# Spreading the splits of the down-projection operands, and handing Strassen sums from bank to bank on ScalarE

## The chip, the core and the metric

The kernel runs on one NeuronCore of a Trainium2 chip. Its engines are TensorE (matrix products, with a separate queue of weight loads), VectorE and ScalarE (elementwise work; both can read and write PSUM, the eight accumulator banks that TensorE writes), GpSimd (here it only issues DMAs) and SyncE (it only issues DMAs). In the rows they are PE, PEld, DVE, ACT, POOL and SP. The metric is the device time of one execution in microseconds, as the median of several runs.

## What is computed

The reference is a trunk of two layers on 1024 tokens of width 1024. Each layer has a mixer (a state-space branch and a windowed attention branch, merged by gates) and then a dense SwiGLU feed-forward part of width 2816:

```
hn2 = rmsnorm(h, norm2_g[layer])
ff = jax.nn.silu(hn2 @ ffn_w_gate[layer]) * (hn2 @ ffn_w_up[layer])
h = h + ff @ ffn_w_down[layer]
```

The change touches this feed-forward part alone.

## The kernel before, in words

**Numbers.** Every fp32 operand is split into a high part, rounded by a ScalarE copy to the type fp32r, and a low part, the rest, by a VectorE subtraction (`split`, `quad_part`, `parts`). A product then takes three matmuls of 128x128 by 128x512: high by high, high by low, low by high. The two token halves are h = 0 and 1, of 512 columns each.

**Quads.** Most of the feed-forward part is done in quads: a 2x2 block product by Strassen's seven products instead of eight. In a gate quad (`quad_items`) the two block rows are the gate and the up weights of one 128-row slice f, the two block columns are the token halves, and each product sums over four 128-deep tiles: 12 matmuls. In a down quad (`down_quad`) the block rows are two neighbouring output slices m and m+1, and the sum runs over half of a chunk of slices f: chunks of 8 give 12 matmuls in a product, chunks of 6 give 9. Layer 0 has 14 gate quads and 4+2 down quads in 2 chunks; layer 1 has 19 gate quads and 4+4+2 down quads in 3 chunks: 33 and 16 in all.

The weights of a quad come as five parts a to e (`quad_part`): a is the upper row as loaded, the others are sums and differences made by VectorE. Parts a and b hold two products' weights, in buffers `whi` and `wlo` (three of each); c, d and e hold one, in slots `whs` and `wls`. The other operands are the tiles of the normalized input with their Strassen sums `T[0]` to `T[3]` (gate quads), or seven sets `b11`, `t0`, `t1`, `b21`, `t2`, `t3`, `b22` of a chunk (down quads).

**Banks.** The seven products of a quad go to PSUM banks named x, y, v and w. Before, their order was x(a), y(b), v(b), x(a), y(c), w(d), v(e), with the first product of the next quad set in ahead of the last. What a bank shares with others was added on VectorE: `first` copies x to an SBUF tile (ScalarE), `second` adds y to it, `third` adds y and v, further adds bring in w and the finished v. All SBUF tiles of 128x512 come from one pool of 86 slots (`A`), all banks from one pool of 8 (`PS`).

**Operands of the down quads.** As a gate quad ends, `keep` and `row` write its results and their Strassen sums to DRAM. Round the start t0 of a chunk (counted in products), `op_load` reads a set back (SyncE's queue) and `op_split` splits it. `SETS` gives the order; the loads were put at t0-12 to t0-2, the splits at t0-4 to t0+2, one set for each product. While a chunk begins, the sets of the one before (or the operands of the gate quads) still hold their slots until their last product.

**Order of work.** `ffn_items` writes out one list of items: products, epilogues, loads and splits. The weights' splits are set in between by a look-ahead (`emit`, `ahead`). From that list a scheduler of the language fixes, before the run, each engine's own order, so engines run their queues in order and wait for one another by semaphores; it may move an instruction ahead of older ones that it thinks will not be ready.

Of the kernel before, what the change touches and what calls it, by code (L numbers as in the profile page):

```python
# [8 lines left out]
F32 = mybir.dt.float32  # L9
F32R = mybir.dt.float32r  # L10
# [3 lines left out]
ADD, SUB, MUL = ALU.add, ALU.subtract, ALU.mult  # L14
# [7 lines left out]
HC = 512  # L22
# [4 lines left out]
CHUNKS = (((8, 8), (16, 6)), ((0, 8), (8, 8), (16, 6)))  # L27
QUAD_FROM = (8, 3)
DOWN_QUADS = 2
SETS = ("b11", "t1", "t0", "b21", "t2", "t3", "b22")  # L30
QUAD_LOOK = 5
NEG = -1e30
EPS = 1e-6
# [65 lines left out]
class Trunk:  # L99
# [85 lines left out]
    def piece(self, ps, g, off, xs, start):  # L185

        from functools import partial
        mm = partial(self.nc.tensor.matmul, skip_group_check=not start)
        for k, (xh, xl) in enumerate(xs):
            s = off + k * P  # L190
            wh, wl = g.hi[:, s:s + P], g.lo[:, s:s + P]
            mm(ps, lhsT=wh, rhs=xh, start=start and k == 0, stop=False)  # L192
            mm(ps, lhsT=wh, rhs=xl, start=False, stop=False)  # L193
            mm(ps, lhsT=wl, rhs=xh, start=False, stop=k == len(xs) - 1)  # L194

    def item(self, fn, *granules):
        self.seq.append((fn, granules))
# [980 lines left out]
    def ffn_items(self, l, fill, head):  # L1178
# [19 lines left out]
        def keep(f, h, x):  # L1198

            if f < grouped:  # L1200
                ff[h][f] = self.split(x, f"ff{f % 6}")
                return
            c, j, k = places[f]
            act[f, h] = x
            if (k, h) != (0, 1) or c == len(chunks) - 1:
                put(c, f"b{k + 1}{h + 1}", j, x)

        def row(f):
            c, j, k = places[f]
# [12 lines left out]
        def op_load(c, kind):  # L1222
            ts = ops[c, kind] = [self.A("fr") for _ in range(chunks[c][1] // 2)]
            for j, t in enumerate(ts):
                nc.sync.dma_start(t, fd[c, kind, j])

        def op_split(c, kind):
            ops[c, kind] = [self.split(t, "fo") for t in ops[c, kind]]

        def gate(f, h, g, st, part=None):  # L1230
            if part != 1:
# [66 lines left out]
        def down_quad(c, m):  # L1298

            f0, n = chunks[c]  # L1300
            w = n * P // 2
            at_end = c == len(chunks) - 1
            q = Quad(*(self.t["w_down"][l, i, :, f0:f0 + n].rearrange("p k c -> p (k c)") for i in (m, m + 1)), w)
            b = {}

            def product(bank, g, off, kind, start):
                def run():
                    if start:
                        b[bank] = self.PS(f"q{bank}")
                    self.piece(b[bank], g, off, ops[c, kind], start)  # L1310
                return (run, g)

            p = [product(*a) for a in (("x", q.a, 0, "b11", True), ("y", q.b, w, "t1", True), ("v", q.b, 0, "t0", True),
                                       ("x", q.a, w, "b21", False), ("y", q.c, 0, "t2", False), ("w", q.d, 0, "t3", True),
                                       ("v", q.e, 0, "b22", False))]

            def out(i, h, x):
                if at_end:
                    last_sum(m + i, h, x)
                else:  # L1320
                    nc.gpsimd.dma_start(self.hs[m + i, h], x, accum_op=ADD)

            def first():
                b["p1"] = self.A("qp")
                nc.scalar.copy(b["p1"], b["x"])

            def second():
                b["u2"] = self.A("qu")
                V.tensor_tensor(b["u2"], b["p1"], b["y"], ADD)

            def c11():
                if at_end:
                    out(0, 0, b["x"])
                    return
                t = self.A("dx")
                nc.scalar.copy(t, b["x"])
                out(0, 0, t)

            def third():
                V.tensor_tensor(b["p1"], b["p1"], b["y"], ADD)  # L1340
                b["c22"] = self.A("qc")
                V.tensor_tensor(b["c22"], b["p1"], b["v"], ADD)
                out(1, 1, b["c22"])

            def c21():
                V.tensor_tensor(b["p1"], b["p1"], b["w"], ADD)
                out(1, 0, b["p1"])

            def c12():
                V.tensor_tensor(b["u2"], b["u2"], b["v"], ADD)  # L1350
                out(0, 1, b["u2"])

            return p, [(fn,) for fn in (first, second, c11, third, c21, c12)]

# [25 lines left out]
        def quad_items(f):  # L1380

            q = Quad(self.t["w_gate"][l, f].rearrange("p k c -> p (k c)"), self.t["w_up"][l, f].rearrange("p k c -> p (k c)"))
            b = {}

            def product(bank, g, off, xs, start):
                def run():
                    if start:
                        b[bank] = self.PS(f"q{bank}")
                    self.piece(b[bank], g, off, xs(), start)
                return (run, g)  # L1390

            B = lambda h, a: lambda: self.hn2[h][a:a + 4]
            p = [product("x", q.a, 0, B(0, 0), True), product("y", q.b, HC, lambda: T[1], True),
                 product("v", q.b, 0, lambda: T[0], True), product("x", q.a, HC, B(0, 4), False),
                 product("y", q.c, 0, lambda: T[2], False), product("w", q.d, 0, lambda: T[3], True),
                 product("v", q.e, 0, B(1, 4), False)]

            def first():
                b["p1"] = self.A("qp")
                nc.scalar.copy(b["p1"], b["x"])  # L1400

            def second():
                b["u2"] = self.A("qu")
                V.tensor_tensor(b["u2"], b["p1"], b["y"], ADD)
# [5 lines left out]
            def third():  # L1410
                V.tensor_tensor(b["p1"], b["p1"], b["y"], ADD)
                b["c22"] = self.A("qc")
                V.tensor_tensor(b["c22"], b["p1"], b["v"], ADD)

            def half0():
                s = b["s0"]
                V.scalar_tensor_tensor(s, s, 1.0, b["x"], ADD, MUL)
                V.tensor_tensor(b["p1"], b["p1"], b["w"], ADD)
                V.scalar_tensor_tensor(s, b["p1"], 0.5, s, MUL, MUL)  # L1419
                keep(f, 0, s)  # L1420

            def gate1():
                V.tensor_tensor(b["u2"], b["u2"], b["v"], ADD)  # L1423
                b["s1"] = self.A("ts")
                nc.scalar.activation(b["s1"], b["u2"], AF.Tanh, scale=0.5)  # L1425

            def half1():
                s = b["s1"]
                V.scalar_tensor_tensor(s, s, 1.0, b["u2"], ADD, MUL)
                V.scalar_tensor_tensor(s, b["c22"], 0.5, s, MUL, MUL)  # L1430
                keep(f, 1, s)
                row(f)

            return p, [(fn,) for fn in (first, second, gate0, third, half0, gate1, half1)]

# [53 lines left out]
        def at(t, fn):  # L1489
            more.setdefault(t, []).append((fn,))  # L1490

        for t0, c in begins:
            for k, kind in enumerate(SETS):
                at(t0 - 12 + k * 17 // 10, lambda c=c, kind=kind: op_load(c, kind))
                at(t0 - 4 + k, lambda c=c, kind=kind: op_split(c, kind))
        c = len(chunks) - 1
        end = 7 * len(made)

# [19 lines left out]

        do(made[0][0][0])
        for i, (p, e) in enumerate(made):  # L1520
            do(p[1])
            main.append(e[0])
            do(p[2])
            main.append(e[1])
            do(p[3])
            do(p[4])
            main.append(e[2])
            do(p[5])
            main.append(e[3])
            if i + 1 < len(made):  # L1530

                do(made[i + 1][0][0])
            main.append(e[4])
            do(p[6])
            main.extend(e[5:])
# [270 lines left out]
```

## Time and profile before

| | us |
|---|---|
| median of 3 runs (2644.98 to 2649.70) | 2648.95 |
| the profiled execution | 2647.83 |
| its span, first to last instruction | 2646.1 |
| TensorE busy in the span | 2564.8 (97%) |
| VectorE busy | 1827.9 (69%) |
| ScalarE busy | 1022.1 (39%) |

The profiled execution took 1.7 us more than its span, and is within 0.1% of the median. Busy shares are averages over stages; matmuls are pipelined, so a busy TensorE says nothing of its rate. Mean granted TensorE clock: 0.986 of full speed.

### The profile page before, as it was taken

The page shows a single profiled execution, that of the slowest core. Times are in us where ns is not written, and L with a number is a line of the kernel's source. Part 1 is how long each engine was busy: PE and PEld are TensorE (multiplying, and loading weights), DVE is VectorE, ACT ScalarE, POOL GpSimd, SP SyncE. Part 2 cuts the span into 40 slices and gives each one's busy share as a digit, 9 for nine tenths or more (in the row PEclk, how much of TensorE's full clock was granted, in tenths as well). Part 3 has the DMA queues.
Part 4 walks back from the last instruction along what each step waited for, and adds up shares of the span by engine and source line. Part 5 has one row for each costly group of instructions (what it writes and reads, how often), then busy time and mean ns, then how long its engine had stood idle before and what let it go on. Part 6 is the DMA issues. An engine that isn't in the chain of part 4 may idle for free.

```text
span 2646.1 us, 35134 instructions
## 1 busy us (share of the span) xinstructions
PE 2564.8 (97%) x12722; PEld 2088.1 (79%) x12722; DVE 1827.9 (69%) x3577; ACT 1022.1 (39%) x1949; POOL 321.3 (12%) x528
## 2 busy tenths in 40 slices
PE   8999899999999999998999999999999999998997
PEld 6787677887888888886787778888878888886776
DVE  9986878575977677677763465756377777676766
ACT  5336744422443333233444553453233222234432
POOL 0141011000142111011100001200001011111110
PEclk9999999999999999998999999999999999998998
DMA  3453435354174533255732244434322233255773
GB/s 139 136 186 118 136 120 180 124 186 140 55 197 132 98 110 108 96 202 137 200 133 76 72 140 161 159 120 167 127 92 93 102 104 116 92 199 156 176 190 123
DMA packets 160510, 357.01 MB, mean 135 GB/s; under 512 B 22048, under 2 KB 44832, under 8 KB 160336
## 3 DMA queue, kind: packets, MB, share of 16 engines
q1 hardware_dynamic: 117136, 236.28, 26.9%
q0 software_dynamic: 43200, 118.48, 15.9%
q8 instruction: 100, 1.64, 0.2%
q14 instruction: 74, 0.61, 0.1%
HBM read 230.97 MB, written 123.68 MB: 134 GB/s over the span
## 4 chain that ended last, share of the span: by engine, by line
PE 88%; DVE 7%; ACT 2%; issue 1%; DMA 1%; SPq 0%; DVEq 0%; ACTq 0%
PE pj L181 6%; PE pj L182 6%; PE pj L183 6%; PE qx L192 3%; PE qx L193 3%; PE qx L194 3%; PE qy L192 3%; PE qy L194 3%; PE qy L193 3%; PE qv L192 3%; PE qv L193 3%; PE qv L194 3%; PE wo L181 2%; PE wo L183 2%; PE wo L182 2%; PE br L181 2%
## 5 line engine op out<-in xcount | busy, mean ns | idle before, releaser
L181 PE MATMUL pj<-rah,whi 128*128 128x512 f32 x768 | 306.2, 399 | 0.4 <-DVE sm L804 0.4
L182 PE MATMUL pj<-ral,whi 128*128 128x512 f32 x768 | 300.1, 391 | 0.7 <-DVE ral L116 0.7
L183 PE MATMUL pj<-rah,wlo 128*128 128x512 f32 x768 | 299.9, 391 | 0.0
L170 DVE TENSOR_TENSOR wlo<-raw,whi 128x1024 fp32r<-128x1024 f32 (+1 forms) x126 | 145.7, 1156 | 168.3 <-ACT whi L169 159.0
L169 ACT CAST whi<-raw 128x1024 fp32r<-128x1024 f32 (+1 forms) x126 | 125.3, 995 | 273.9 <-PE pj L182 115.1
L181 PEld LDWEIGHTS pj<-rah,whi 128*128 128x128 f32 x768 | 144.7, 188 | 35.4 <-issue 4.7
L182 PEld LDWEIGHTS pj<-ral,whi 128*128 128x128 f32 x768 | 144.8, 189 | 30.9 <-DVE ral L116 2.6
L183 PEld LDWEIGHTS pj<-rah,wlo 128*128 128x128 f32 x768 | 144.5, 188 | 30.8
L1425 ACT ACTIVATE ts<-qu 128x512 f32<-128x512 f32 x33 | 20.9, 633 | 287.2 <-DVE qu L1423 287.2
L804 DVE CUSTOM_DVE_ANT_0 x<-s,bias,nsink 128x384 f32<-128x384 f32 (+1 forms) x128 | 67.5, 581 | 64.0 <-PE s L798 63.9
L1423 DVE TENSOR_TENSOR qu<-qu,qv 128x512 f32<-128x512 f32 x33 | 22.7, 687 | 125.8 <-PE qv L194 125.8
L192 PE MATMUL qx<-rfh,whi 128*128 128x512 f32 x264 | 102.7, 389 | 0.0
L193 PE MATMUL qx<-rfl,whi 128*128 128x512 f32 x264 | 102.7, 389 | 0.0
L194 PE MATMUL qx<-rfh,wlo 128*128 128x512 f32 x264 | 102.7, 389 | 0.0
L976 ACT COPY s5sg<-s5s 64x256 f32<-64x256 f32 x128 | 51.7, 404 | 128.8 <-DVE s5s L971 127.4
L181 PE MATMUL wo<-mgh,whi 128*128 128x512 f32 x256 | 100.0, 391 | 0.0
L1196 POOL DMA_DIRECT2D fd_b<-ts x60 | 32.6, 543 | 553.4 <-DVE ts L1419 464.2
L183 PE MATMUL wo<-mgh,wlo 128*128 128x512 f32 x256 | 99.7, 389 | 0.0
L182 PE MATMUL wo<-mgl,whi 128*128 128x512 f32 x256 | 99.6, 389 | 0.0
L157 ACT CAST whs<-s 128x512 fp32r<-128x512 f32 (+1 forms) x98 | 59.9, 612 | 99.3 <-DVE s L150 93.3
L157 ACT CAST whi<-sm 128x1024 fp32r<-128x1024 f32 (+1 forms) x49 | 50.6, 1033 | 122.7 <-PE qv L193 102.9
L158 DVE TENSOR_TENSOR wlo<-sm,whi 128x1024 fp32r<-128x1024 f32 (+1 forms) x49 | 58.9, 1202 | 41.8 <-ACT whi L157 41.7
(468 smaller groups left out, 7191.0 us busy)
## 6 DMA issues: line engine op xcount, KB each, us to landing
raw<-in_w_in SPq DMA_DIRECT2D x52, 512.0 KB
raw<-in_w_gate SPq DMA_DIRECT2D x44, 512.0 KB
raw<-in_w_up SPq DMA_DIRECT2D x44, 512.0 KB
fd_t<-ft POOLq DMA_DIRECT2D x72, 256.0 KB, 2.7
fr<-fd_t SPq DMA_DIRECT2D x72, 256.0 KB
g<-th POOLq DMA_DIRECT2D x64, 256.0 KB, 2.8
thr<-g SPq DMA_DIRECT2D x64, 256.0 KB
fd_b<-ts POOLq DMA_DIRECT2D x60, 256.0 KB, 2.3
```

The costliest lines, as they stand in the source:

```text
L157: nc.scalar.copy(g.hi[:, n], src)
L158: V.tensor_tensor(g.lo[:, n], src, g.hi[:, n].bitcast(F32), SUB)
L169: nc.scalar.copy(g.hi[:, :n], g.raw[:, :n])
L170: nc.vector.tensor_tensor(g.lo[:, :n], g.raw[:, :n], g.hi[:, :n].bitcast(F32), SUB)
L181: mm(ps, lhsT=wh, rhs=xh, start=k == 0, stop=False)
L182: mm(ps, lhsT=wh, rhs=xl, start=False, stop=False)
L183: mm(ps, lhsT=wl, rhs=xh, start=False, stop=k == n - 1)
L192: mm(ps, lhsT=wh, rhs=xh, start=start and k == 0, stop=False)
L193: mm(ps, lhsT=wh, rhs=xl, start=False, stop=False)
L194: mm(ps, lhsT=wl, rhs=xh, start=False, stop=k == len(xs) - 1)
L804: V.tensor_tensor_reduce(out=x[:, :n], in0=ps[:, :n], in1=self.bias[hd][:, bo:bo + n], op0=ADD, op1=ALU.min, scale=-1.0, scalar=self.nsink ...
L976: nc.scalar.copy(SG[64 * r:64 * r + 64, g * 256:(g + 1) * 256].rearrange("p (d n) -> p d n", d=2), Sv[64 * g:64 * g + 64, :, r])
```

## The change

Four edits, all in the feed-forward part.

1. A loaded operand tile is split in place: the tile that the DMA filled becomes the low part, so a split takes one new slot, not two with the loaded one freed later.
2. The seven sets are taken in the order in which the products use them; loads go to t0-14 to t0-2 and splits to t0-10 to t0+3 by two explicit lists, 13 products from the first split to the last instead of 6.
3. Each quad has five banks x, v, y, z, w. ScalarE copies x into y before T1's product accumulates on it, then y into z and v into an SBUF tile, then y into w. The products accumulate on these copies. VectorE is left with one add for c22 and one for c12 (or the up value of half 1).
4. The order of products is x, v, y, x, y, z, (next x), w, and the epilogues are moved with it: c21 and half 0 come last.

```diff
-SETS = ("b11", "t1", "t0", "b21", "t2", "t3", "b22")
+SETS = ("b11", "t0", "t1", "b21", "t2", "b22", "t3")
+LOADS = (-14, -10, -8, -7, -5, -4, -2)
+SPLITS = (-10, -6, -4, -2, 0, 2, 3)
...
+    def carry(self, b):
+        nc, V = self.nc, self.nc.vector
+        def first():
+            b["y"] = self.PS("qy")
+            nc.scalar.copy(b["y"], b["x"])
+        def second():
+            b["z"] = self.PS("qz")
+            nc.scalar.copy(b["z"], b["y"])
+            b["sv"] = self.A("qp")
+            nc.scalar.copy(b["sv"], b["v"])
+        def third():
+            b["w"] = self.PS("qw")
+            nc.scalar.copy(b["w"], b["y"])
+            b["c22"] = self.A("qc")
+            V.tensor_tensor(b["c22"], b["sv"], b["y"], ADD)
+        return first, second, third
...
-            ts = ops[c, kind] = [self.A("fr") for _ in range(chunks[c][1] // 2)]
+            ts = ops[c, kind] = [self.A("fol", F32R) for _ in range(chunks[c][1] // 2)]
...
-            ops[c, kind] = [self.split(t, "fo") for t in ops[c, kind]]
+            for lo in ops[c, kind]:
+                hi = self.A("foh", F32R)
+                nc.scalar.copy(hi, lo.bitcast(F32))
+                V.tensor_tensor(lo, lo.bitcast(F32), hi.bitcast(F32), SUB)
...
-("y", q.b, w, "t1", True), ("v", q.b, 0, "t0", True),
-("x", q.a, w, "b21", False), ("y", q.c, 0, "t2", False), ("w", q.d, 0, "t3", True), ("v", q.e, 0, "b22", False)
+("v", q.b, 0, "t0", True), ("y", q.b, w, "t1", False),
+("x", q.a, w, "b21", False), ("y", q.c, 0, "t2", False), ("z", q.e, 0, "b22", False), ("w", q.d, 0, "t3", False)
...
             def c21():
-                V.tensor_tensor(b["p1"], b["p1"], b["w"], ADD)
-                out(1, 0, b["p1"])
+                if at_end:
+                    out(1, 0, b["w"])
+                    return
+                t = self.A("dx")
+                nc.scalar.copy(t, b["w"])
+                out(1, 0, t)
...
             def half0():
                 V.scalar_tensor_tensor(s, s, 1.0, b["x"], ADD, MUL)
-                V.tensor_tensor(b["p1"], b["p1"], b["w"], ADD)
-                V.scalar_tensor_tensor(s, b["p1"], 0.5, s, MUL, MUL)
+                V.scalar_tensor_tensor(s, b["w"], 0.5, s, MUL, MUL)
                 keep(f, 0, s)
+                row(f)
...
-            for k, kind in enumerate(SETS):
-                at(t0 - 12 + k * 17 // 10, lambda c=c, kind=kind: op_load(c, kind))
-                at(t0 - 4 + k, lambda c=c, kind=kind: op_split(c, kind))
+            for kind, a, b in zip(SETS, LOADS, SPLITS):
+                at(t0 + a, lambda c=c, kind=kind: op_load(c, kind))
+                at(t0 + b, lambda c=c, kind=kind: op_split(c, kind))
```

## Rows read from the trace of the kernel before

**Rows 1.** The page: busy us, share of the span and instructions of each engine.
```profile
PE 2564.8 (97%) x12722; PEld 2088.1 (79%) x12722; DVE 1827.9 (69%) x3577; ACT 1022.1 (39%) x1949; POOL 321.3 (12%) x528
```
**Rows 2.** TensorE's waits, whole span: us in total, times, longest.
```profile
PE qw L193 <- DVE fol L116: 14.8, 5, 6.3
PE qw L192 <- ACT foh L115: 13.5, 5, 3.2
...
PE qv L192 <- DVE qc L1413: 5.5, 2, 2.8
```
**Rows 3.** Timeline of TensorE, start of layer 0's first chunk: start, duration, [idle before].
```profile
1202.22 0.39 PE L194 MATMUL qv<-foh,wlo 128*128 128x512 f32 x1
1205.37 0.78 PE L192 MATMUL qv<-rfh,whs 128*128 128x512 f32 x1 [2.77 <-DVE qc L1413]
...
1212.00 0.60 PE L192 MATMUL qw<-foh,whs 128*128 128x512 f32 x1 [2.01 <-ACT foh L115]
1218.84 0.79 PE L193 MATMUL qw<-fol,whs 128*128 128x512 f32 x1 [6.24 <-DVE fol L116]
...
1224.30 0.39 PE L194 MATMUL qw<-foh,wls 128*128 128x512 f32 x1
```
**Rows 4.** Windows: length; busy (instructions) PE, PEld, DVE, ACT, POOL; clock, DMA share, GB/s.
```profile
908.00:1099.00 191.00, 191.00 (x844) 158.19 (x844) 139.17 (x200) 61.00 (x93) 22.89 (x37) 1.00 0.39 113
1202.22:1224.30 22.08, 11.07 (x31) 7.89 (x30) 19.03 (x31) 11.01 (x21) 3.25 (x6) 0.69 0.30 112
1294.34:1304.53 10.19, 6.38 (x15) 4.37 (x14) 8.38 (x14) 6.92 (x13) 0.00 (x0) 0.67 0.50 125
2389.66:2411.92 22.26, 11.14 (x32) 8.00 (x30) 19.23 (x31) 11.01 (x21) 3.25 (x6) 0.69 0.31 112
2484.01:2494.27 10.26, 6.18 (x20) 4.41 (x18) 10.17 (x17) 7.28 (x14) 0.86 (x1) 0.83 0.22 27
2564.31:2574.41 10.10, 6.29 (x16) 4.28 (x14) 8.38 (x14) 6.92 (x13) 0.00 (x0) 0.66 0.54 143
```
**Rows 5.** Timeline of ScalarE, the same start of layer 0's first chunk.
```profile
1202.42 1.04 ACT L157 CAST whi<-sm 128x1024 fp32r<-128x1024 f32 x1 [2.79 <-PE qv L193]
1203.37 2.17 ACT L115 CAST foh<-fr 128x512 fp32r<-128x512 f32 x4
```
**Rows 6.** Timeline of VectorE, the same start.
```profile
1203.49 1.22 DVE L158 TENSOR_TENSOR wlo<-sm,whi 128x1024 fp32r<-128x1024 f32 x1 [2.29 <-ACT whi L157]
1204.63 0.68 DVE L1413 TENSOR_TENSOR qc<-qp,qv 128x512 f32<-128x512 f32 x1
...
1218.10 2.49 DVE L116 TENSOR_TENSOR fol<-fr,foh 128x512 fp32r<-128x512 f32 x4
```
**Rows 7.** Windows of two gate quads and of two down quads.
```profile
1099.00:1137.00 38.00, 38.00 (x170) 31.46 (x169) 27.70 (x41) 10.71 (x16) 4.33 (x8) 1.00 0.33 112
1233.00:1271.00 38.00, 38.00 (x170) 31.46 (x168) 20.17 (x28) 10.21 (x16) 6.86 (x8) 1.00 0.80 190
```
**Rows 8.** Groups by line and shape: busy us, mean ns, idle before.
```profile
L157 ACT CAST whi<-sm 128x1024 fp32r<-128x1024 f32 x45 | 47.3, 1051 | 95.4 <-PE qv L193 91.4 <-issue 2.6 <-PE dn L182 1.4
L1400 ACT COPY qp<-qx 128x512 f32<-128x512 f32 x33 | 18.8, 569 | 1.4 <-PE qx L194 1.4
L157 ACT CAST whi<-sm 128x768 fp32r<-128x768 f32 x4 | 3.3, 836 | 27.2 <-issue 15.7 <-PE qv L193 11.5
```
**Rows 9.** Timeline of TensorE: the last matmul of one gate quad's first product.
```profile
1101.40 0.39 PE L194 MATMUL qx<-rfh,wlo 128*128 128x512 f32 x1
```
**Rows 10.** Timeline of ScalarE in that gate quad.
```profile
1105.27 0.63 ACT L1425 ACTIVATE ts<-qu 128x512 f32<-128x512 f32 x1 [9.26 <-DVE qu L1423]
1105.80 0.57 ACT L1400 COPY qp<-qx 128x512 f32<-128x512 f32 x1
```
**Rows 11.** Waits of SyncE's DMA queue, whole span.
```profile
SPq L1225 <- PE qy L194: 6.7, 6, 2.3
SPq L1225 <- PE qx L194: 4.9, 5, 1.7
```

More of the change, by code (lines that the diff above doesn't have):

```diff
@@ L1222, in op_load @@
         def op_load(c, kind):
-            ts = ops[c, kind] = [self.A("fr") for _ in range(chunks[c][1] // 2)]
+            ts = ops[c, kind] = [self.A("fol", F32R) for _ in range(chunks[c][1] // 2)]
             for j, t in enumerate(ts):
-                nc.sync.dma_start(t, fd[c, kind, j])
+                nc.sync.dma_start(t.bitcast(F32), fd[c, kind, j])
         def op_split(c, kind):
-            ops[c, kind] = [self.split(t, "fo") for t in ops[c, kind]]
+            pairs = []
+            for lo in ops[c, kind]:
+                hi = self.A("foh", F32R)
+                nc.scalar.copy(hi, lo.bitcast(F32))
+                V.tensor_tensor(lo, lo.bitcast(F32), hi.bitcast(F32), SUB)
+                pairs.append((hi, lo))
+            ops[c, kind] = pairs
         def gate(f, h, g, st, part=None):
@@ L1311, in product @@
                 return (run, g)
-            p = [product(*a) for a in (("x", q.a, 0, "b11", True), ("y", q.b, w, "t1", True), ("v", q.b, 0, "t0", True),
-                                       ("x", q.a, w, "b21", False), ("y", q.c, 0, "t2", False), ("w", q.d, 0, "t3", True),
-                                       ("v", q.e, 0, "b22", False))]
+            p = [product(*a) for a in (("x", q.a, 0, "b11", True), ("v", q.b, 0, "t0", True), ("y", q.b, w, "t1", False),
+                                       ("x", q.a, w, "b21", False), ("y", q.c, 0, "t2", False), ("z", q.e, 0, "b22", False),
+                                       ("w", q.d, 0, "t3", False))]
             def out(i, h, x):
@@ L1321, in out @@
                     nc.gpsimd.dma_start(self.hs[m + i, h], x, accum_op=ADD)
[L1323 to L1329, printed above, removed]
+            first, second, carry = self.carry(b)
             def c11():
@@ L1339, in third @@
             def third():
-                V.tensor_tensor(b["p1"], b["p1"], b["y"], ADD)
-                b["c22"] = self.A("qc")
-                V.tensor_tensor(b["c22"], b["p1"], b["v"], ADD)
+                carry()
                 out(1, 1, b["c22"])
             def c21():
-                V.tensor_tensor(b["p1"], b["p1"], b["w"], ADD)
-                out(1, 0, b["p1"])
+                if at_end:
[4 more added lines that the diff above has]
+                out(1, 0, t)
             def c12():
-                V.tensor_tensor(b["u2"], b["u2"], b["v"], ADD)
-                out(0, 1, b["u2"])
+                u = self.A("qu")
+                V.tensor_tensor(u, b["sv"], b["z"], ADD)
+                out(0, 1, u)
             return p, [(fn,) for fn in (first, second, c11, third, c21, c12)]
@@ L1392, in quad_items @@
             B = lambda h, a: lambda: self.hn2[h][a:a + 4]
[L1393 to L1404, printed above, removed]
+            p = [product("x", q.a, 0, B(0, 0), True), product("v", q.b, 0, lambda: T[0], True),
+                 product("y", q.b, HC, lambda: T[1], False), product("x", q.a, HC, B(0, 4), False),
+                 product("y", q.c, 0, lambda: T[2], False), product("z", q.e, 0, B(1, 4), False),
+                 product("w", q.d, 0, lambda: T[3], False)]
+            first, second, third = self.carry(b)
             def gate0():
@@ L1408, in gate0 @@
                 nc.scalar.activation(b["s0"], b["x"], AF.Tanh, scale=0.5)
[L1410 to L1413, printed above, removed]
             def half0():
@@ L1417, in half0 @@
                 V.scalar_tensor_tensor(s, s, 1.0, b["x"], ADD, MUL)
[L1418 to L1419 removed]
+                V.scalar_tensor_tensor(s, b["w"], 0.5, s, MUL, MUL)
                 keep(f, 0, s)
+                row(f)
             def gate1():
[L1423 removed]
+                b["u2"] = self.A("qu")
+                V.tensor_tensor(b["u2"], b["sv"], b["z"], ADD)
                 b["s1"] = self.A("ts")
@@ L1431, in half1 @@
                 keep(f, 1, s)
-                row(f)
             return p, [(fn,) for fn in (first, second, gate0, third, half0, gate1, half1)]
@@ L1520, in ffn_items @@
         for i, (p, e) in enumerate(made):
+            main.append(e[0])
             do(p[1])
-            main.append(e[0])
             do(p[2])
@@ L1525, in ffn_items @@
             do(p[3])
+            main.append(e[2])
             do(p[4])
-            main.append(e[2])
+            main.append(e[3])
             do(p[5])
-            main.append(e[3])
             if i + 1 < len(made):
                 do(made[i + 1][0][0])
-            main.append(e[4])
+            main.append(e[5])
             do(p[6])
-            main.extend(e[5:])
+            main.extend(e[6:] + [e[4]])
         assert not more, more.keys()
```

## The prediction

> **What bounds the kernel now.** I read the page's busy shares first, then TensorE's waits, then a timeline where those waits lie, and last windows over each of them. TensorE is busy for 97% of the span [rows 1], so only the time in which it stands still or runs slowly can be won; the change takes no matmul away. Of the waits, the longest belong to one place: the first product on bank w, five times on VectorE's low parts and five times on ScalarE's high parts, and twice product v of the last gate quad [rows 2]. Together 14.8 + 13.5 + 5.5 = 33.8 us. Five is the number of chunk starts.
>
> One start in detail: TensorE begins its last full-speed matmul at 1202.22, waits 2.77, 2.01 and 6.24 us, and is back at full pace at 1224.30 [rows 3]. The reader is to see that matmuls after a wait come slower too (0.78 and 0.79 us against 0.39). So I price a start by its whole stretch. In a steady stretch 844 matmuls take 191.00 us, 0.226 each, at clock 1.00; in the five stretches 30, 14, 30, 18 and 14 began (the weight loads count them), at clocks 0.66 to 0.83 [rows 4]. At the steady pace they need 6.79, 3.17, 6.79, 4.07 and 3.17 us; they took 22.08, 10.19, 22.26, 10.26 and 10.10. Lost: 15.3 + 7.0 + 15.5 + 6.2 + 6.9 = 50.9 us, of which 33.8 is waiting and 17.1 the slower clock behind it. That is 1.9% of the run, and the ceiling of what the change can win there.
>
> Why TensorE waits: VectorE works 19.03 of the 22.08 us [rows 4] and still ends splits of a set at 1220 [rows 6]. In the rest of its time it is blocked by order: ScalarE's cast of part b can't start before TensorE lets its buffer go (1202.42, [rows 5]); VectorE's `wlo` waits 2.29 us for that cast; and the add c22, for which TensorE waits, stands behind it [rows 6].
>
> **The spread of the splits.** A product of 12 matmuls takes 12 x 0.226 = 2.72 us, one of 9 takes 2.04. Four splits take VectorE 2.49 us [rows 6], a start's seven sets 17.4. Two gate quads keep VectorE busy 27.70 of 38 us, 73%; two down quads 20.17, 53% [rows 7]. Old plan, from t0-4 to t3's product at t0+7: 11 products or 29.9 us, demand 10.9 x 0.73 + 19.0 x 0.53 + 17.4 = 35.4. It is 5.5 us short, and blocking adds to that. New plan, from t0-10 to t0+7: 17 products or 46.2 us. VectorE loses three adds in each quad; at some 0.60 us each (four splits in 2.49 us give 0.60 from start to start) two quads fall to 24.1 and 16.6 us, 63% and 44%. Demand 27.2 x 0.63 + 19.0 x 0.44 + 17.4 = 42.9: it fits, at 93%. With the old adds it would be 27.2 x 0.73 + 19.0 x 0.53 + 17.4 = 47.3 and would not: the two halves of the change need each other. In the densest part, t0-6 to t0+4, six sets fall in 27.2 us: 14.9 + 16.3 x 0.63 + 10.9 x 0.44 = 30.0, 2.8 us over; each set is used three to nine products after its split is listed, so I cost this at nothing. Without that lead it is 2.8 us at each of the two starts behind gate quads, 5.6.
>
> The wait on c22 goes away for another reason: no product accumulates on v once it has been read, so TensorE needs nothing of that add.
>
> **The copies.** ScalarE gets three more copies a quad (z, the saved v, w), and one for c21 in the 12 down quads that aren't at the end: 3 x 49 + 12 = 159. A copy from PSUM to SBUF takes 0.569 us [rows 8]. From PSUM to PSUM no row shows; bounds are 0.48 (four casts in 2.17 us, 0.52 apart [rows 5], less the copy's 0.05) and 1.05, the cast of twice the size [rows 8]. I take 0.57, the nearest row; 91 us in all on an engine that is busy 39% [rows 1]. Beside the splits: two gate quads rise from 10.71 to 14.1 us of 38, two down quads from 10.21 to about 14.8 [rows 7]; in the 46.2 us round a start 27.2 x 0.37 + 19.0 x 0.39 + 7 x 2.18 = 32.8, 71%. It fits.
>
> What counts is not load but lateness, as TensorE now waits for these copies. x into y has the products w and v as cover, 5.4 us; y into w has z and the next x, 5.4 us; y into z has only the second x product, 2.72 us (2.04 in the last chunks), since T2's product overwrites y. Ahead of it stands one cast of part a or b, whose buffer comes free with the same product: 1.05 + 0.57 = 1.62 us, under 2.72; in the small chunks 0.84 + 0.57 = 1.41, under 2.04 [rows 8]. With the upper price of the copy 2.10 and 1.89, still under. So in a steady quad the copies cost nothing, and the work that hides them is the one product in between; without that cover each costs its 0.57 to 1.05.
>
> At a start the set b22 is listed right behind the first quad's y product, in front of this copy: 4 casts in 2.17, 1.05 and 0.57 make 3.79 us, 1.07 over; for 3 tiles 3 x 0.52 + 0.10 + 0.84 + 0.57 = 3.07, 1.03 over. Five starts: 3 x 1.07 + 2 x 1.03 = 5.3 us. Below it, nothing, if the scheduler sets the copy first. I double it to 10 for the orders that a busy share can't show.
>
> **Order, queues and memory.** The loads are as many as before, 28 or 21 a start, and stand in SyncE's queue with the weights' loads. Some already wait for a slot, 6.7 us in six cases and 4.9 in five, at most 2.3 us [rows 11]. By my count of slots the old operands hold 56 of 86; with loads and splits in place the new plan reaches 72 at t0-7 (the old one 68 at t0-9), and the quads' own tiles take about 20 more. So some loads will wait for a product to end: one or two products late, and the weights' loads queued behind them with them, whose buffers hold a quad ahead (19 us). Nothing, on a lead of three to nine products; if it costs, it is the partial case below. `row` moves behind half 0, some 1.2 us later, and its writes in GpSimd's queue with it; they are read several quads later. c21 at the end reads its bank directly, an add fewer.
>
> **Sum.** 50.9 - 10 = 41 us less. The profiled execution's 2647.8 would become 2607; the median of the runs stands 1.1 us above that execution, so 2648.95 becomes 2608. The bounds: nothing left at the starts, 2598; 20 left, 2618.
>
> **Rivals.**
>
> *Half of the loss stays.* The slots are the limit, loads come late, and splits pile up before t0 again. For it: the slot count above, and a VectorE at 93%. Against: loads wait at most 2.3 us today. Half of 50.9 is 25: 2623, in a range of 2618 to 2643.
>
> *Slower: ScalarE's y-to-z copy comes late in every quad.* Today's copy of x starts at 1105.80, though its product's last matmul ended at 1101.79: 4.0 us late, because it stands behind the tanh of the quad before, and that waits for VectorE [rows 9, 10]. The Trainium skill, "TensorE: Matmul & The Clock Gate" (Architectural detail: the array is 16× 32×32), says that ScalarE and VectorE take their queues strictly first in, first out; this row is such a case, and by that rule alone a copy is as late as the worst instruction listed ahead of it. If the new copy is as late, TensorE waits 4.0 + 0.57 - 2.72 = 1.85 us in each of 49 quads, 91 us: 2608 + 91 = 2699. It decides from 41 / 49 = 0.84 us a quad, a copy that starts 3.0 us after its product. Against it: the tanh that blocks today is moved a product earlier, ahead of the copies, and the adds that it waits for meet a VectorE with three instructions less.
>
> *Banks run out.* A quad now takes five of eight banks, not four. The Trainium skill, "PSUM — Partial Sum Buffer" (Summary: rules for kernel authors), asks to empty banks promptly, as they are few; no wait of TensorE here shows a lack of banks so far. Counted by order, at most seven live at once: x, z and w of one quad, then x, y, v of the next and one spare. If v's bank must wait for half 0 of the quad before, two instructions of VectorE after w at some 0.68 us [rows 6], it is about 1.3 us a quad: 2608 + 64 = 2672.
>
> *No change.* The starts stay as they are because the orders, not the load, make them, or new waits eat the gain: about 2649.
>
> **How the numbers follow.** This kernel's runs can tell 0.2%, 5.3 us, from no change. Forecast (2598 to 2618) 0.65, half stays 0.16, no change 0.07, late copies 0.10, banks 0.02. Faster 0.65 + 0.16 = 0.81; same 0.07; slower 0.12. The range leaves the slower cases out above, and runs from 2597 to 2646; the forecast's own is 2598 to 2618.
>
> **What would show it.** Right: no wait on `fol` or `foh` over 1 us among TensorE's waits, the wait on `qc` gone, the clock 1.00 through the starts, VectorE's busy time down by about 147 x 0.69 = 101 us and ScalarE's up by about 91. Wrong: a wait of products y, z or w on the lines of `carry`, once in each quad (late copies); waits of bank v or x on VectorE's half 0 (banks); splits still under way on VectorE after t0+4, with loads that wait on TensorE for several us (slots).

## The result, and the profile after

The changed kernel takes 2605.55 us (median of 4 runs, 2604.12 to 2607.86), the one before beside it 2649.32: a ratio of 0.9838, interval 0.9821 to 0.9855. That is 43.8 us less, where 41 were forecast. The profiled execution's span fell from 2646.1 to 2603.6 us, by 42.5, and its mean granted clock rose from 0.986 to 0.995.

The page of the changed kernel, in the form of [rows 1]:

```profile
PE 2546.7 (98%) x12722; PEld 2076.1 (80%) x12722; DVE 1730.4 (66%) x3430; ACT 1111.5 (43%) x2108; POOL 322.5 (12%) x528
```

VectorE lost 147 instructions and 97.5 us, ScalarE got 159 more and 89.4 us; 101 and 91 were forecast. TensorE's waits, as in [rows 2] (us in total, times, longest):

```profile
PE psn L335 <- DVE sqc L326: 3.5, 2, 2.4
PE qz L196 <- DVE fol L1258: 2.3, 2, 1.2
...
PE qy L195 <- ACT qz L209: 1.5, 2, 0.7
```

These are all the waits of quad products that are left: 3.8 us where 33.8 stood. The wait on `qc` is gone. The line on `psn` is the norm's reduction at the end of a feed-forward part; before, it showed 2.5 us, once. The windows (columns as in [rows 4]) of the start of layer 0's first chunk, the start of its second one, and of that reduction:

```profile
1184.00:1214.50 30.50, 29.34 (x130) 23.99 (x129) 28.14 (x43) 21.29 (x37) 3.74 (x8) 1.00 0.61 215
1276.00:1290.00 14.00, 13.26 (x58) 10.62 (x57) 9.12 (x15) 8.01 (x16) 1.72 (x3) 1.00 0.69 185
1324.00:1333.30 9.30, 8.15 (x37) 6.57 (x36) 4.55 (x17) 1.38 (x3) 1.09 (x2) 0.82 0.36 122
```

The reader is to see the clock: 1.00 at both starts, where it was 0.69 and 0.67 [rows 4], and 0.82 in a place that no step of the prediction spoke of. The first start in detail, on TensorE and then on VectorE:

```profile
1210.19 0.39 PE L195 MATMUL qz<-foh,whs 128*128 128x512 f32 x1
1211.73 0.50 PE L196 MATMUL qz<-fol,whs 128*128 128x512 f32 x1 [1.16 <-DVE fol L1258]
```

```profile
1205.71 0.68 DVE L1240 TENSOR_TENSOR ft<-ts 128x512 f32<-128x512 f32 x1
1206.32 1.22 DVE L161 TENSOR_TENSOR wlo<-sm,whi 128x1024 fp32r<-128x1024 f32 x1
...
1208.66 0.68 DVE L1243 TENSOR_TENSOR ft<-ts,ft 128x512 f32<-128x512 f32 x1
1209.26 0.68 DVE L149 TENSOR_TENSOR s<-raw,sm 128x512 f32<-128x512 f32 x1
1209.86 1.22 DVE L161 TENSOR_TENSOR wlo<-raw,whi 128x1024 fp32r<-128x1024 f32 x1
1211.00 4.90 DVE L1258 TENSOR_TENSOR fol<-fol,foh 128x512 fp32r<-128x512 f32 x8
```

One wait of 1.16 us is left of 2.77, 2.01 and 6.24 [rows 3], and the matmuls behind it soon come at 0.39 again. It is for the low parts of b22, which stand on VectorE behind the four adds of `row` (L1240 to L1243), two weight splits and a weight's difference. The same 1.16 us stands at layer 1's first start. In the small chunks the queue is the one that the prediction wrote down, first ScalarE, then TensorE:

```profile
1280.33 0.84 ACT L160 CAST whi<-sm 128x768 fp32r<-128x768 f32 x1 [3.31 <-PE qy L196]
1281.08 1.65 ACT L1257 CAST foh<-fol 128x512 fp32r<-128x512 f32 x3
1282.63 0.58 ACT L209 COPY qz<-qy 128x512 f32<-128x512 f32 x1
```

```profile
1282.13 0.39 PE L197 MATMUL qx<-foh,wlo 128*128 128x512 f32 x1
1283.26 0.50 PE L195 MATMUL qy<-foh,whs 128*128 128x512 f32 x1 [0.74 <-ACT qz L209]
```

Cast of part b, three casts of b22, then the copy y to z: together 2.88 us from 1280.33 to 1283.21, and TensorE stands 0.74 us. The prediction had 3.07 us and 1.03. The copies by groups (busy us, mean ns):

```profile
L211 ACT COPY qp<-qv 128x512 f32<-128x512 f32 x49 | 28.7, 586 | 160.2 <-PE qv L197 158.2 <-issue 2.1
L209 ACT COPY qz<-qy 128x512 f32<-128x512 f32 x49 | 28.4, 580 | 2.1 <-PE qy L197 2.1
...
L205 ACT COPY qy<-qx 128x512 f32<-128x512 f32 x49 | 28.0, 571 | 58.8 <-PE qx L197 58.6
```

From bank to bank a copy takes 0.571 to 0.580 us; 0.57 was taken, between bounds of 0.48 and 1.05. Last, the loads that wait for a slot, in SyncE's queue as in [rows 11]:

```profile
SPq L1250 <- PE qy L197: 2.5, 7, 0.8
...
SPq L1250 <- PE qx L196: 1.2, 1, 1.2
```

They wait less than before, at most 1.2 us against 2.3. In the changed kernel the slots are no limit.

### The profile page after: what moved, and what is told of

It is laid out like the page before. It is cut to its first block, busy times and chain, and to the rows that moved or that the text cites. A ratio compares the mean times of both kernels' runs of the same rounds, so it can differ in the third digit from the quotient of the medians.

```text
span 2603.6 us, 35062 instructions
## 1 busy us (share of the span) xinstructions
PE 2546.7 (98%) x12722; PEld 2076.1 (80%) x12722; DVE 1730.4 (66%) x3430; ACT 1111.5 (43%) x2108; POOL 322.5 (12%) x528
## 4 chain that ended last, share of the span: by engine, by line
PE 89%; DVE 7%; ACT 2%; DMA 1%; issue 1%; SPq 0%; DVEq 0%; ACTq 0%
PE pj L184 6%; PE pj L185 6%; PE pj L186 6%; PE qy L195 3%; PE qx L196 3%; PE qx L195 3%; PE qx L197 3%; PE qy L196 3%; PE qy L197 3%; PE br L184 2%; PE br L186 2%; PE wo L184 2%; PE br L185 2%; PE wo L185 2%; PE wo L186 2%; PE qz L196 2%
## 5 line engine op out<-in xcount | busy, mean ns | idle before, releaser
L211 ACT COPY qp<-qv 128x512 f32<-128x512 f32 x49 | 28.7, 586 | 160.2 <-PE qv L197 158.2
L1258 DVE TENSOR_TENSOR fol<-fol,foh 128x512 fp32r<-128x512 f32 x132 | 82.7, 685 | 13.8 <-ACT foh L1257 13.8
L325 ACT ACTIVATE sq<-h 128x512 f32<-128x512 f32 x56 | 35.3, 631 | 118.5 <-DVE h L1172 67.9
```

Of the source, the lines that this page charges most:

```text
L1258: V.tensor_tensor(lo, lo.bitcast(F32), hi.bitcast(F32), SUB)
```

## The experiments

All times are medians of 4 runs; the kernel before, run beside them on the same chips, took 2647.3 or 2647.53 us. "Times" means the new lists of loads and splits, "in place" the split into the loaded tile, "copies" the bank copies with all that belongs to them (banks, order of products, moved epilogues, order of the sets).

Two theories stood against each other. By that of **load**, which the prediction used, the starts were lost because VectorE had more work round them than time; then the new times and the adds taken off VectorE are the gain, each needs the other, and the split in place is worth nothing. By that of **path**, TensorE lost time because what it waited for stood deep in VectorE's queue; then it matters which engine writes what TensorE needs next and what is listed ahead of it, and VectorE's busy share does not.

### Which edit brings how much

**The kernel before with times and in place, without copies** (`e1_plan_inplace`; the lists `LOADS` and `SPLITS` are those of the change, the sets keep their old order):

```diff
-            ts = ops[c, kind] = [self.A("fr") for _ in range(chunks[c][1] // 2)]
+            ts = ops[c, kind] = [self.A("fol", F32R) for _ in range(chunks[c][1] // 2)]
...
-            ops[c, kind] = [self.split(t, "fo") for t in ops[c, kind]]
+            pairs = []
+            for lo in ops[c, kind]:
+                hi = self.A("foh", F32R)
+                nc.scalar.copy(hi, lo.bitcast(F32))
+                V.tensor_tensor(lo, lo.bitcast(F32), hi.bitcast(F32), SUB)
+                pairs.append((hi, lo))
+            ops[c, kind] = pairs
...
-            for k, kind in enumerate(SETS):
-                at(t0 - 12 + k * 17 // 10, lambda c=c, kind=kind: op_load(c, kind))
-                at(t0 - 4 + k, lambda c=c, kind=kind: op_split(c, kind))
+            for kind, a, b in zip(SETS, LOADS, SPLITS):
+                at(t0 + a, lambda c=c, kind=kind: op_load(c, kind))
+                at(t0 + b, lambda c=c, kind=kind: op_split(c, kind))
```

> The kernel before with the new load and split times and the split in place, but the old four banks, the old order of products and sets, and VectorE's adds. Theory A (VectorE's budget needs both halves): demand 47.3 us in 46.2 round a start, so most of the split waits go, but the add c22 still holds product v at the two starts behind gate quads (2 x 2.8 us and the slower clock behind them) and some split waits stay: 2612 to 2625 us. Theory B (the plan of the splits is all of it, the copies are idle): within 0.2% of the changed kernel, 2601 to 2610. Theory C (the orders, not the load, make the waits): 2635 or more.

Measured: 2614.42 us, 0.9875 [0.9858, 0.9891]. The time is inside the 2612 to 2625 of theory A, the waits are not its own. No product waits for `fol` or `foh` any more; two other waits have come, twice each (TensorE's waits, then VectorE at the first start):

```profile
PE qy L194 <- DVE qu L1338: 8.6, 2, 4.3
...
PE qx L194 <- ACT qp L1334: 3.4, 2, 1.7
```

```profile
1209.19 0.68 DVE L1220 TENSOR_TENSOR ft<-ts,ft 128x512 f32<-128x512 f32 x1
1209.80 0.68 DVE L148 TENSOR_TENSOR s<-raw,sm 128x512 f32<-128x512 f32 x1
1210.40 2.49 DVE L1235 TENSOR_TENSOR fol<-fol,foh 128x512 fp32r<-128x512 f32 x4
1212.81 0.68 DVE L1338 TENSOR_TENSOR qu<-qp,qy 128x512 f32<-128x512 f32 x1
```

The splits are early enough now; bank y isn't free, as the add that reads it (`second`, L1338) stands behind the last add of `row` (L1220), a weight's sum and four splits. TensorE waits 4.31 us for it.

**Times alone** (`e2_plan_only`: the last part of that diff).

> As the one before but with the loaded tile and two new tiles for each split, as in the kernel before: only the load and split times are changed. If slots are no limit: the same as that one within 0.2%. If slots limit the early splits: slower by 5 us or more, with loads on SyncE's queue waiting longer for products.

Measured: 2633.88 us, 0.9949 [0.9934, 0.9964]. The same kind of wait, and the one on `qc` longer than before:

```profile
PE qv L194 <- DVE qc L1415: 9.3, 2, 4.6
...
PE qy L194 <- DVE qu L1331: 5.3, 2, 2.7
```

It is 19.5 us slower than with the split in place, and the second case of the expectation holds: loads wait for slots. The longest such line of SyncE's queue:

```profile
SPq L1227 <- PE qv L196: 16.0, 8, 4.8
```

With the split in place the same line is 5.8 us in two. So with the old banks and the new times slots are a limit, and the split in place relieves it; how much of the 19.5 us that makes, no run tells.

**In place alone** (`e9_inplace_only`: the first two parts of that diff).

> The kernel before with the split in place alone: old banks, orders, load and split times. By the table so far, the split in place was worth 19 us beside the new times in the old banks, and 6 to 8 us beside the copies. If it works by freeing slots for earlier splits, it needs no new times to do so: 2618 to 2632 us, with the waits of product w on foh and fol shorter and those on VectorE's adds left. Rival (it needs the early loads to be of use): 2642 or more.

Measured: 2619.52 us, 0.9895 [0.988, 0.991]: 28.0 us from an edit that has no term in the sum. The waits that are left lie at the two starts behind gate quads (4.14 and 3.51 us at the first); at the three others no product waits, and none waits for `qc`.

```profile
PE qw L192 <- ACT foh L1232: 8.3, 2, 4.1
...
PE qw L193 <- DVE fol L1233: 7.0, 2, 3.5
```

What the traces show is another order in the queues. ScalarE at layer 0's second chunk, first in the kernel before, then here:

```profile
1294.59 0.83 ACT L157 CAST whi<-sm 128x768 fp32r<-128x768 f32 x1 [7.87 <-issue]
...
1295.74 3.21 ACT L115 CAST foh<-fr 128x512 fp32r<-128x512 f32 x6
```

```profile
1282.95 3.24 ACT L1232 CAST foh<-fol 128x512 fp32r<-128x512 f32 x6
...
1291.83 0.84 ACT L157 CAST whi<-sm 128x768 fp32r<-128x768 f32 x1 [5.16 <-PE qv L193]
```

The six casts of t2 and t3 stood behind a cast of part b that came after 7.87 us of idle time, and TensorE waited 3.23 us for one of them; with the split in place they stand ahead of it. At the first chunk's start the add into `qc` comes at 1201.68, ahead of the split `wlo` (1209.49), where it stood behind it [rows 6].

**Copies alone** (`e3_carry_only`): the changed kernel with the old times and `self.split(t, "fo")` into new tiles.

```diff
-            ts = ops[c, kind] = [self.A("fol", F32R) for _ in range(chunks[c][1] // 2)]
+            ts = ops[c, kind] = [self.A("fr") for _ in range(chunks[c][1] // 2)]
...
+            ops[c, kind] = [self.split(t, "fo") for t in ops[c, kind]]
...
-            for kind, a, b in zip(SETS, LOADS, SPLITS):
-                at(t0 + a, lambda c=c, kind=kind: op_load(c, kind))
-                at(t0 + b, lambda c=c, kind=kind: op_split(c, kind))
+            for k, kind in enumerate(SETS):
+                at(t0 - 12 + k * 17 // 10, lambda c=c, kind=kind: op_load(c, kind))
+                at(t0 - 4 + k, lambda c=c, kind=kind: op_split(c, kind))
```

> The changed kernel with the old load and split times and without the split in place: only the five banks, ScalarE's copies and the order of products and sets. Theory A: no wait on c22; VectorE's demand 32.6 us in 29.9 from t0-4 to t0+7, against 35.4 before, so 2 to 4 us of split waits a start stay at the starts behind gate quads and less at the others: 2615 to 2632 us. Theory B: copies idle, the same as before, 2644 to 2654. Rival of late copies: slower than before.

Measured: 2611.47 us, 0.9868 [0.9853, 0.9882], better than expected. The splits are late here, but by little:

```profile
PE qy L196 <- DVE fol L119: 6.1, 9, 1.4
```

**Copies and times, not in place** (`e4_two_tiles`: the first two parts of the diff above).

> The changed kernel without the split in place alone: each split takes two new tiles and frees the loaded one. Theory A (lead hides late slots): within 0.2% of the changed kernel, 2601 to 2610. Rival (slots limit): 2612 or more, with foh casts later against the products and waits on fol or foh of more than 1 us a start.

Measured: 2611.6 us, 0.9865 [0.9851, 0.988], outside the 2601 to 2610 expected by theory A and 0.4 us short of its rival's 2612. ScalarE's high parts are waited for 4.9 us in two places, VectorE's low parts 3.0 us in four.

**Copies and in place, old times** (`e5_carry_inplace`: the last part of that diff).

> The changed kernel with the old load and split times alone (five banks, copies, new orders and the split in place stay). Theory now, after the first four: early splits are worth only what the slots let them be, and the copies take VectorE's adds out of TensorE's way. Then the old times still crowd VectorE (32.6 us of work in 29.9 at the starts behind gate quads): waits on foh and fol of 2 to 5 us a start, 2608 to 2613 us. Rival (the times do nothing once a split takes one new tile): within 0.2% of the changed kernel, 2600 to 2610, with at most 4 us of waits at all five starts together.

Measured: 2603.82 us, 0.9834 [0.9819, 0.9849]; of the products only y waits:

```profile
PE qy L195 <- ACT qz L209: 2.4, 3, 0.8
```

Here the 2608 to 2613 expected by the theory of load fell. With its rows the table of the three edits is full:

| times | in place | copies | us |
|---|---|---|---|
| - | - | - | 2647.3 to 2649.3 |
| yes | - | - | 2633.88 |
| - | yes | - | 2619.52 |
| yes | yes | - | 2614.42 |
| - | - | yes | 2611.47 |
| yes | - | yes | 2611.60 |
| - | yes | yes | 2603.82 |
| yes | yes | yes | 2605.55 |

The new times, which name the change, bring some 13 us alone, 5 beside in place, and nothing that these runs can tell once the copies are there. Copies alone bring 36 us, in place alone 28, both 44: they overlap by 20. In place alone clears the three starts that have no gate quads behind them, 7.0 + 6.2 + 6.9 = 20.1 us [rows 4], and cuts the waits at the two others from 11.0 us [rows 3] to 4.14 + 3.51 = 7.65.

### Load or path

**VectorE gets its work back, off the path** (`e8_vector_load`): three adds more in each quad, into a tile that nothing reads; the computation is otherwise unchanged.

```diff
             nc.scalar.copy(b["sv"], b["v"])
+            V.tensor_tensor(self.scr, b["sv"], b["sv"], ADD)
...
             V.tensor_tensor(b["c22"], b["sv"], b["y"], ADD)
+            V.tensor_tensor(self.scr, b["sv"], b["c22"], ADD)
+            V.tensor_tensor(self.scr, b["sv"], b["c22"], ADD)
...
```

> The changed kernel with three adds on VectorE put back in each quad, on SBUF tiles alone and into an unused tile, so nothing waits for them: the old VectorE load without the old path. Load theory (the budget: 47.3 us of work in 46.2 round a start): waits on split parts come back at the starts, 2 to 6 us each, 2612 to 2630. Path theory (what the copies win is that TensorE no longer waits for an add): within 0.2% of the changed kernel, 2601 to 2611.

Measured: 2604.45 us, 0.9837 [0.9822, 0.9851]. VectorE is back at the number of instructions of [rows 1] and within 10 us of its busy time, and the time stays (b22's low parts are waited for 3.0 us, not 2.3):

```profile
PE 2546.7 (98%) x12722; PEld 2076.0 (80%) x12722; DVE 1818.4 (70%) x3577; ACT 1111.7 (43%) x2108; POOL 321.4 (12%) x528
```

**The bank copies on VectorE** (`e12_carry_vector`): the same products and banks, but what TensorE waits for stands in VectorE's queue again.

```diff
-            nc.scalar.copy(b["y"], b["x"])
+            V.tensor_copy(b["y"], b["x"])
...
-            nc.scalar.copy(b["z"], b["y"])
+            V.tensor_copy(b["z"], b["y"])
...
-            nc.scalar.copy(b["w"], b["y"])
+            V.tensor_copy(b["w"], b["y"])
```

> The changed kernel with the three bank-to-bank copies on VectorE instead of ScalarE (v's copy into SBUF stays on ScalarE). Path theory (what counts is which queue TensorE waits behind, and VectorE's is the one that is crowded at a start): waits of products y, z or w on these copies return at the starts, 2 to 6 us each, 2615 to 2640 us. Rival (a copy early enough is as good on either engine): within 0.2% of the changed kernel, 2600 to 2611.

Measured: 2612.4 us, 0.9867 [0.9852, 0.9881], just under the range expected. VectorE is as busy as in the run above (1815.5 us), yet 8 us are lost, mostly by two waits of 4.0 us at the starts behind gate quads. VectorE and TensorE at the first of them:

```profile
1206.94 0.69 DVE L1240 TENSOR_TENSOR ft<-ts 128x512 f32<-128x512 f32 x1
...
1210.48 0.68 DVE L149 TENSOR_TENSOR s<-raw,sm 128x512 f32<-128x512 f32 x1
1211.08 0.69 DVE L209 COPY qz<-qy 128x512 f32<-128x512 f32 x1
```

```profile
1204.79 0.39 PE L197 MATMUL qy<-foh,wlo 128*128 128x512 f32 x1
...
1211.92 0.76 PE L195 MATMUL qy<-foh,whs 128*128 128x512 f32 x1 [4.02 <-ACT foh L1257]
```

The row names ScalarE's `foh` as the releaser. But in the changed kernel the same product starts at 1207.47 and the last casts of `foh` near it at 1208.41 and 1210.96, so it doesn't read those. Here TensorE starts 0.15 us after the copy's end at 1211.77, and that copy started 5.9 us after the product that it reads ended (1205.18), behind `row` and weight work. So I read the copy as what was waited for, against the row's attribution. The Trainium skill, "TensorE: Matmul & The Clock Gate" (Architectural detail: the array is 16× 32×32), says that VectorE and ScalarE run their queues strictly first in, first out; this row agrees: a copy of 0.69 us waited 5.9 us with its input ready.

**What these runs don't separate.** This run still wins 35.1 of the 42 us over the kernel before beside it, so the engine of the copies is a small part. The traces show one thing more that the copies change: TensorE's own order. Before, T3's product on w is listed behind the second x product and T2's product on y. At all five starts the scheduler let TensorE begin it ahead of both, and the 14.8 and 13.5 us of [rows 2] are waits of that product for the set listed last but one. At the first start TensorE begins w at 1212.00 [rows 3], and these only then:

```profile
1220.71 0.63 PE L192 MATMUL qx<-foh,whi 128*128 128x512 f32 x1
...
1226.12 0.39 PE L192 MATMUL qy<-foh,whs 128*128 128x512 f32 x1
```

With the copies, T3's product accumulates on what T2's has left and can't be taken ahead. How much of the copies' 36 us is this order, and how much the adds taken off the path, no run tells.

### How much room the new copies have

**Two and four copies more on ScalarE ahead of y to z** (`e6_delay2`, shown here, and `e11_delay4` with `range(4)`), into a tile that nothing reads; the computation is otherwise unchanged.

```diff
+            for _ in range(2):
+                nc.scalar.copy(self.scr, b["y"])
             b["z"] = self.PS("qz")
             nc.scalar.copy(b["z"], b["y"])
...
```

> The changed kernel with two more ScalarE copies of bank y into an unused SBUF tile ahead of the copy y into z, in all 49 quads: it comes some 1.05 us later, and everything else stays. By the slack of the prediction (2.72 less 1.62, or 1.10 us, in products of 12 matmuls; 0.63 in the 4 quads of 9) the quads with 12 hold just about and those of 9 wait 0.4 us each: 0 to 10 us slower than the changed kernel, 2605 to 2616. Rival (no such slack, because ScalarE's queue is blocked by other things): about 1 us in each quad, 40 us or more slower, 2645 or more.

> The changed kernel with four more ScalarE copies of y ahead of the copy y into z, some 2.1 us in all 49 quads. Two used up the slack and added 9 us (half of it 0.08 us a quad); two more must now be paid for in full: some 1.05 us a quad, 51 us more than with two, 2655 to 2675 us, slower than before the change, with a wait on the copy in every quad. Rival (the scheduler finds TensorE other work, or ScalarE's order hides it): 2615 to 2640.

Measured: 2612.4 us, 0.9865 [0.9848, 0.9881], with two; 2679.3 us, 1.0119 [1.0104, 1.0134], with four, slower than before and slightly over the range expected. One line of TensorE's waits from each:

```profile
PE qy L195 <- ACT qz L211: 5.3, 5, 2.2
```

```profile
PE qy L195 <- ACT qz L211: 60.3, 49, 4.2
```

ScalarE's busy time rose by 51.6 us for the 98 copies and by 100.5 for the 196: the copy y to z comes 1.05 us later in a quad, or 2.05. The first is just taken up by the slack of 1.10 us, but for five waits; the second brings a wait in each of the 49 quads, 1.02 us in most, so the slack measures 2.05 - 1.02 = 1.03. This is the rival of late copies made on purpose. It cost 73.8 us against the changed kernel for 58.8 us more of this wait; the 42.0 us that the change had won beside these runs would be gone at 42.0 / 73.8 x 58.8 / 49 = 0.68 us a quad. The prediction put that point at 0.84, without the clock that waits cost.

### Slots

**82 slots instead of 86** (`e10_slots82`: `N_SLOTS = 82`). A split in place saves one tile for each of a set's four operands while it runs.

> The changed kernel with 82 slots in the pool instead of 86, 4 fewer, which is what a set of 4 takes more for a while when it isn't split in place. Slot theory: the same loss as without the split in place, 2608 to 2616 us, with foh casts late in the same way. Rival (it is something else in the split, such as its order on ScalarE): within 0.2% of the changed kernel, 2600 to 2611 with an unchanged list of waits.

Measured: 2601.85 us, 0.9827 [0.981, 0.9843], with the same waits of products, 2.3 us in two on `fol` and 1.5 in two on `qz`. Four slots fewer cost nothing, so beside the copies four slots saved are not the reason why the split in place helps. With the old banks this was not run.

### A better version

**b22 split one product earlier** (`e7_b22_early`), so that it is not listed between the first y product and the copy y to z:

```diff
-SPLITS = (-10, -6, -4, -2, 0, 2, 3)
+SPLITS = (-10, -6, -4, -2, 0, 1, 3)
```

> The changed kernel with the split of set b22 listed one product earlier (t0+1 instead of t0+2), so ahead of the product y and not between it and the copy y into z. Theory: the waits on that copy in the two small chunks (0.74 us each) and on b22's low parts (1.16 us each behind the gate quads) go; 2602 to 2605 us, not to be told from the changed kernel by time, only by the waits. Rival (these waits come from VectorE's load, not from the list): they stay or move to another product.

Measured: 2597.95 us (2596.98 to 2599.85), 0.9813 [0.9799, 0.9828], the fastest of all and below the 2602 to 2605 expected. No product of a quad waits at all, and the second wait on `psn` is gone too:

```profile
PE psn L335 <- DVE sqc L326: 2.4, 1, 2.4
```

Its profiled span is 2596.6 us, 7.0 below the changed kernel's and 49.5 below that of before: the ceiling of 50.9 is nearly reached. Counted from matmul to matmul, 4.3 of the 7.0 us lie in the quads and 2.6 at the norm's reduction.

## Why the prediction was right, and where not

**The ceiling and the wait on `qc`.** Right. The 50.9 us of [rows 3, 4] were there to be won, the slower clock with them: the starts run at 1.00, and the version with b22 earlier wins 49.5. `qc` is no longer waited for, as no product accumulates on v. The sum rests on this ceiling and not on the budget that follows it, so the forecast held though the reason given for it did not; that much is luck.

**The step that failed: the spread of the splits.** It budgeted VectorE's time (35.4 us of work in 29.9, then 42.9 in 46.2) and concluded that the two halves of the change need each other. The new times alone bring 13 us, nothing beside the copies, and VectorE given its adds back costs nothing. So, with the copies there, neither the longer spread nor the relief of VectorE is needed while the other is there; a run with neither was not made. What the runs show in its place is the path. With the old banks TensorE waits behind VectorE's queue (4.3 us on `qu` with early splits); with ScalarE's copies it doesn't; with the same copies on VectorE it does again (4.0 us, on a copy 5.9 us late). That choice of engine is shown, and is 2612.4 - 2605.55 = 6.9 of the 44 us; for the rest the path is an argument, as banks, adds and orders changed together. The budget also ends the old stretch with t3's product at t0+7. In the old list that product stands at t0+5, and TensorE took it two products earlier still, which the reading of the first start missed. A demand over the stretch's length says that somebody will be late; it doesn't say that TensorE is the one who waits.

**The second step that failed: no term for the split in place.** It is worth 28.0 us alone and about 8 beside the copies (2611.47 to 2603.82). Only its slots were counted, not the order of each engine that comes of it. That the orders come out otherwise is shown, on ScalarE and on VectorE; why the scheduler sets them so is open. Four slots are not the reason beside the copies. With the old banks slots are a limit to the new times, and whether they also set the order under the old times was not run.

**The copies.** Right in price (0.571 to 0.580 us), in number (159), in the slack (1.10 us by the working, 1.03 by the run with four copies more), and in the queue in the small chunks, down to the order cast, three casts, copy. Mis-sized was what it leaves: 10 us were kept for five starts, and 3.8 are lost at four, 1.16 twice and 0.74 twice. At the big chunks it is not the copy that is late but b22's low parts, behind `row` on VectorE.

**The sum.** 50.9 less 3.8 is 47.1, and the span fell by 42.5: 4.6 us were given back elsewhere. Of these 2.9 are at the end of layer 0's feed-forward part:

```profile
1325.55 1.05 PE L335 MATMUL psn<-ones,sqc 128*128 128x1 f32 x8 [1.15 <-DVE sqc L326]
1326.46 0.61 PE L1324 MATMUL dn<-foh,whs 128*128 128x512 f32 x1
...
1332.26 1.05 PE L358 MATMUL psn<-cst,rs 128*128 128x128 f32 x8
```

TensorE now reaches the norm's reduction before VectorE has the squares, 1.15 us; the 18 matmuls behind it then take 5.80 us (1326.46 to 1332.26) instead of 18 x 0.226 = 4.07. Counted from matmul to matmul, the quads gained 20.0 and 26.2 us, 0.9 less than 47.1, in part by slower matmuls behind the four waits that are left. The output's last DMAs are waited for 2.7 us at the end instead of 1.6, which no edit touches. So the forecast of 41 was near 43.8 partly because two errors offset each other: a residue at the starts that was too large by 6.2, and a loss elsewhere that it had not.

**The rivals.** Half of the loss did not stay: the loads wait at most 1.2 us for a slot. Late copies were the true danger; the time of two copies was the margin. No product waits for VectorE's half 0, so the banks did not run out. The orders, which the prediction named under "No change", did make the waits in part, but the change alters them too.

## What to carry to other kernels

Price a wait by what stands ahead of its releaser in that engine's queue, not by the engine's busy share, and read the critical engine's own order from the trace, not from the list. Put what the critical engine needs next on the engine with the short queue, write down the slack (one product less what stands ahead, here 1.10 us), and list bulky work ahead of the handover, not between a product and its copy. Before a change of several edits is credited to the one that names it, run the edits singly; here the named one was worth nothing beside the others, and one line of the plan more was worth 7.6 us. When a long wait goes, look for the next place where the faster engine comes too early.

## What the runs showed of the hardware

A wait of about one microsecond did not slow TensorE's clock at the starts, longer ones did. Three windows of the run with four extra copies:

```profile
1165.00:1226.00 61.00, 57.97 (x252) 47.06 (x252) 46.38 (x69) 36.95 (x65) 5.95 (x11) 1.00 0.63 216
1289.00:1295.00 6.00, 5.90 (x19) 4.69 (x20) 1.74 (x5) 2.33 (x6) 0.85 (x1) 0.72 0.76 188
1311.00:1317.00 6.00, 5.49 (x13) 4.34 (x14) 2.57 (x5) 2.50 (x5) 0.00 (x0) 0.51 0.73 253
```

The first stretch holds three waits of 1.02 us, one in each quad, and the clock is 1.00 throughout, the level of 2.4 GHz. The second follows a wait of 2.18 us and the third one of 4.17; 0.51 is the level of 1.2 GHz nearly all the time. In the changed kernel the 1.15 us before `psn`, with eight matmuls of one column behind it, was followed by 0.82. So the 30.0 us of waits taken away brought most of their clock with them: the quads gained 46.2 us, 16.2 more than the waits, of the 17.1 priced.

Writing a bank costs ScalarE about what writing SBUF does: 571 to 580 ns for the copies into y, w and z, against 586 for the one of v into SBUF and 569 for the old one of x [rows 8]. The Trainium skill, "ScalarE: Activation LUTs" (Step-by-step: what each stage is for), says that ScalarE writes to PSUM faster than to SBUF; these rows don't show it, as the times into SBUF lie on both sides.
